# An order of issue that counts table loads, the first Silu behind the last norm, and one operand split on two engines

## The chip, the cores and the metric

The kernel runs on one core of a Trainium2 chip. A core has five engines with queues of their own: TensorE (PE, with its weight loads as PEld), VectorE (DVE), ScalarE (ACT), GpSimd (POOL) and SyncE (SP), which here issues all the DMAs. The metric is the device time of one execution in microseconds (us). The time before is the median of three runs, 3001.66 us (2999.66 to 3004.17). Each trace is one further execution, taken by the hardware profiler.

## The reference

One layer of a streaming encoder, for 2048 prompt tokens and 32 sample tokens of width 1024, in float32. Both groups share the weights, so the kernel treats them as 2080 columns of one transposed matrix.

```python
x = x + rmsnorm(concat(band_attention, gla) @ w_o)       # 8 heads x 64 | 4 heads x 128, gated
x = x + rmsnorm(softmax(rmsnorm(x) @ w_mq @ k.T) @ v @ w_mo)   # 256 memory tokens, 4 heads
x = x + rmsnorm((silu(h @ w_gate) * (h @ w_up)) @ w_down)      # h = rmsnorm(x), hidden 2816
```

`band_attention` is softmax attention of each 64-token chunk over itself and the eight chunks before; `gla` is a gated linear recurrence. Every `rmsnorm(x)` is `x * rsqrt(mean(x * x) + eps) * gain`. The kernel computes the reciprocal root as Exp(-0.5 * Ln(mean + eps)), so a norm needs ScalarE's Ln and Exp; the feed-forward part needs its Silu.

## The kernel before

**Stages.** The input projection (to about 550 us in the trace) works on three blocks of columns. Then attention and the linear recurrence run beside the output projections of earlier blocks. For the output projection the columns are cut into four blocks `BLK` of 512, 512, 512 and 544. Blocks 0 to 2 are projected while later blocks are still in attention; block 3 comes after all attention (about 1150 to 1235 us). Cross-attention follows: scores from 1235 us, and the outputs of eight tiles of 256 columns from about 1410 us. The feed-forward stage starts at about 1625 us and runs over three pairs of column blocks and eleven groups `g` of 256 hidden units, with seven-product forms of the matrix products in gate, up and down.

**Split operands.** The float32 products on PE are made of three fp32r matmuls (`mm3`): each operand is split into a high part, ACT's cast, and a low part, the difference, which DVE or POOL makes. `split` (lines 459 and 460) does this for weights. `split_own` (464 and 465) does it in place, and its second argument picks POOL or DVE for the low part. `load_mov` (line 1098) loads the eight pieces of an output-projection operand (`om`, 128 rows each) from the DRAM buffer `od` and splits them with `split_own(..., True)`, all on POOL.

**The output projection.** `out_proj(b)` (1431) returns three lists of steps: `first` loads and splits the operand, `tile_m` makes one of eight output tiles from `wops` matmuls (1426), and the last list does the norm and the residual. The pieces are taken in the order 4 to 7, 0 to 3: rows 4 to 7 of `od` come from the recurrence (`od<-g_sg`), rows 0 to 3 from attention (`od<-o`, `od<-so`). `score_weights` (1667) prepares the weights for cross-attention's scores: it loads `gs` from `gd` and combines and splits them on ACT, DVE and POOL. It is called ahead of block 3's `first`.

**Cross-attention's norms.** `output(i, pT)` (1839) makes a tile's output with matmuls `mo`, squares and sums it (`n_q`, `n_s`), and calls `rstd` twice, for the norm after cross-attention and for the one before the feed-forward part. `rstd` (1854) is a matmul of ones, an Ln (1858) and an Exp (1859). The scaled rows (`my`, 1868) are stored to `x2d` and `h2d`.

**The feed-forward units.** `gate_up(g)` (2134) makes the gate product with `unit` (PSUM tiles `pg_X`, `pg_Y`, `pg_Z`), applies four Silus (2140), one of them straight from `pg_X`, makes the up product (`pu_X` and so on, to three buffers `up`) and multiplies (2143). At the last column block a preload brings ScalarE's set for Ln and Exp back ahead of the final norm.

**What sets the order.** The order of instructions in each queue is written out by a planner, the class `Order`. `_read` (191) reads the traced instructions, gives each a cost by `_cost`, and collects what it depends on. `_pass` (287) runs a list schedule over the five engines with the tiles' buffers as limits, which it counts by tag. `queue` (403) makes eleven such passes forwards and ten backwards, each taking its priorities from the one before, keeps the shortest and ties the instructions of each engine into that order. ScalarE's functions live in sets, and a table load stands ahead of an activation whose set isn't in place; the planner before doesn't know of these loads.

Of the kernel before, what the change touches and what calls it, by code (L numbers as in the profile page):

```python
# [18 lines left out]
P = 128  # L19
# [28 lines left out]
class Order:  # L48
# [9 lines left out]
    SLOW = 1.0  # L58
    PASSES = 10
    TURN = 280.0  # L60
    ROOM = (208 * 1024, 16 * 1024)

    def __init__(self, tc):
        self.tc = tc
        self.block = tc.nc.cur_bb
        self.edge = mybir.DependencyInfo(mybir.DependencyClass.NoSync, mybir.DependencyReason.DATA)

    @staticmethod
# [122 lines left out]
    def _read(self, traced):  # L191

        self.ops, self.eng, self.dur, self.lat, self.lane, self.prio = [], [], [], [], [], []
        self.pred, self.uses, tile_of = [], [], {}
        self.tiles = []
        log = []
        opened, closed, owner = {}, {}, {}
# [9 lines left out]
        for ins in traced:  # L207
            kind = type(ins).__name__
            eng = str(ins.engine).split(".")[-1]
            if ins.name in opened:  # L210
                p, space, size, right = opened[ins.name]
                lo = max([q[2] for q in stack.values() if q[0] == space and not q[3]], default=0)
                if right:
                    lo = min([q[1] for q in stack.values() if q[0] == space and q[3]], default=self.ROOM[space == PSUM]) - size
                stack[p] = (space, lo, lo + size, right)
                before = [q for q, (s, a, b) in gone.items() if s == space and a < lo + size and lo < b]
                if before:
                    gate[p] = len(self.ops)
                    form = None
                    self._add(None, self.GATE, (0.0, 0.0), 0, 0, sorted({i for q in before for i in inside.get(q, ())}), [])  # L220
            elif ins.name in closed:
                space, lo, hi, _ = stack.pop(closed[ins.name])
                gone = {q: v for q, v in gone.items() if not (v[0] == space and lo <= v[1] and v[2] <= hi)}
                gone[closed[ins.name]] = (space, lo, hi)
            if kind in ("BassTilePoolBoundary", "InstLoadActFuncSet") or eng not in self.ENGINES:
                continue
            outs = [a.bass_ap for a in ins.outs if hasattr(a, "bass_ap")]
            inps = [a.bass_ap for a in ins.ins if hasattr(a, "bass_ap")]
            was, form = form, self._form(eng, outs, inps)
            joined = form is not None and form == was  # L230
            i = len(self.ops) - joined
            pred, use = set(), []
            for aps, wr in ((inps, False), (outs, True)):
                for ap in aps:
                    t = ap.tensor
                    if type(t).__name__ != "Tile":
                        continue
                    k = tile_of.get(t.name)
                    if k is None:
                        k = tile_of[t.name] = len(self.tiles)  # L240
                        self.tiles.append(t)
                        log.append([])
                    if t.space == PSUM:
                        p0, p1, bits, wr_ = 0, P, 1, True
                    else:
                        p0, p1, bits = self._cells(ap)
                        wr_ = wr
                    keep = []
                    for e in log[k]:
                        j, w, q0, q1, b = e  # L250
                        if j != i and (wr_ or w) and q0 < p1 and p0 < q1 and b & bits:
                            pred.add(j)
                        if not (wr_ and j != i and p0 <= q0 and q1 <= p1 and not b & ~bits):
                            keep.append(e)
                    keep.append((i, wr_, p0, p1, bits))
                    log[k] = keep
                    if t.space != DRAM and k not in use:
                        use.append(k)
                        p = owner.get(t.name)
                        inside.setdefault(p, []).append(i)  # L260
                        if p in gate:
                            pred.add(gate[p])
            cost = self._cost(ins, kind, eng, outs, inps)
            if joined:
                self._join(ins, cost, ins.bass_priority, pred, use)
                continue
            if form is not None:
                cost = cost[0] + self.TURN, cost[1]
            self._add(ins, self.ENGINES.index(eng), cost, self._lane(kind, eng, outs + inps), ins.bass_priority, sorted(pred), use)
        n = len(self.ops)  # L270
        self.succ = [[] for _ in range(n)]
# [15 lines left out]
    def _pass(self, prio, back=None):  # L287

        n = len(self.ops)
        eng, dur, lat, lane = self.eng, self.dur, self.lat, self.lane  # L290
        taken = [0.0] * 3
        nxt, prv = (self.succ, self.pred) if back is None else (self.pred, self.succ)
        left = [len(x) for x in prv]
        live = [k for k in range(len(self.tiles)) if self.first[k] is not None]
# [28 lines left out]
        while True:  # L323
            again = True
            while again:
                again = False
                for e, heap in enumerate(ready):
                    while idle[e] and heap:
# [22 lines left out]
                        idle[e] = False  # L351
                        start[i] = now
                        fin = now + dur[i]
                        if lane[i]:
                            fin = max(fin, taken[3 - lane[i]] + dur[i] - 140.0)
                            taken[lane[i]] = fin
# [42 lines left out]
                            parked[g] = []  # L399
        assert done == n, "the order does not work out"  # L400
        return start, end

    def queue(self):
        self._read(self.block.bb.instructions)
# [25 lines left out]
def encoder_step(ctx, tc, ins, outs):  # L430
# [641 lines left out]
    with ExitStack() as ph, ExitStack() as dn:  # L1072
# [22 lines left out]
            return xps[-1].tile([P, 1088], F32, tag="xw", name=name)  # L1095


        def load_mov(src, n, name, order=range(KT)):
            mv = {}
            for k in order:  # L1100
                mv[k] = mp.tile([P, 2, 544], F32R, tag="mov", name=f"{name}_{k}")
                SP.dma_start(mv[k][:, 1, :n].bitcast(F32), src[k * P : (k + 1) * P])
                split_own(mv[k][:, :, :n], True)
            return mv

        def split_k(ks, kraw):
# [321 lines left out]
                    yield  # L1428


        def out_proj(b):
            s, n = BLK[b]
            chunks = even_split(n, 512)
            mv, y, ys, accs = {}, [], [], []
            order = (4, 5, 6, 7, 0, 1, 2, 3)

            def first():
                mv.update(load_mov(od[b], n, f"om{b}", order))
                y.extend(xtile(f"y1_{b}_{j}")[:, : 2 * n].rearrange("p (k n) -> p k n", k=2) for j in range(4))
                ys.extend(y[k // 2][:, k % 2] for k in range(KT))  # L1440
                accs.append(xtile(f"acc1_{b}")[:, : 2 * n].rearrange("p (k n) -> p k n", k=2))
# [225 lines left out]
        def score_weights():  # L1667
# [3 lines left out]
            for k in range(HK):  # L1671
                b11, b12, b22, b21 = (gst.tile([P, 512], F32, tag="gst", name=f"gs{kh}{hf}_{k}") for kh, hf in ((0, 0), (0, 1), (1, 1), (1, 0)))
                for t, (kh, hf) in zip((b11, b12, b22, b21), ((0, 0), (0, 1), (1, 1), (1, 0))):
                    SP.dma_start(t, gd[kh][hf][:, k * 512 : k * 512 + 512])

                def put(i, src, eng=None):
                    split(gT[i][:, 0, k], gT[i][:, 1, k], src, eng)
# [9 lines left out]
                sub(DVE, b21, b21, b11)  # L1687
                SP.dma_start(s6d[:, k * 512 : k * 512 + 512], b21)

        score_weights()  # L1690
        for _ in steps(outp[3][0] + weave(outp[3][1], [partial(values_fold, 2)] + [partial(values_fold, 3)], lead=1.0)):
            pass
        psx.close()
        amm.close()
# [134 lines left out]
        def softmax(pr, ps, n, st, heads):  # L1829
# [5 lines left out]
            for h in range(heads):  # L1835
                c = slice(h * NMEM, h * NMEM + NMEM)
                DVE.tensor_scalar(out=pr[:n, c], in0=pr[:n, c], scalar1=st[:n, 4 + h : 5 + h], scalar2=None, op0=ALU.mult)

        def output(i, pT):
            t0 = i * 256  # L1840
            y = [yp.tile([P, HK, 256], F32, tag="y", name=f"my{i}_{j}") for j in range(2)]
# [10 lines left out]
                    add(DVE, ssq[nm], ssq[nm], sq)  # L1852

            def rstd(nm):
                r = (pd.tile([P, 512], F32, tag="dense", name=f"{nm}{i}") if nm == "n3_" else ptr.tile([P, 512], F32, tag="tr", name=f"{nm}{i}"))[:, :256]
                add(DVE, ssq[nm][:, 0], ssq[nm][:, 0], ssq[nm][:, 1])
                PE.matmul(r, lhsT=ones, rhs=ssq[nm][:, 0], start=True, stop=True)
                ACT.activation(r, r, AF.Ln, bias=eps_t, scale=1.0 / D)
                ACT.activation(r, r, AF.Exp, scale=-0.5)
                return r  # L1860

            def store(dst, m2):
# [151 lines left out]
    with ExitStack() as ph:  # L2014
# [116 lines left out]
        for b, (s, n) in enumerate(CF):  # L2131
            ssqs, silu = {}, []

            def gate_up(g):
                u = gt.tile([P, 2, 2, 348], F32, tag="g", name=f"g{b}_{g}")[:, :, :, :n]
                sg = {q: u[:, q[0], q[1]] for q in QS}
                up = {q: small(up_, "up", f"up{b}_{g}_{q[0]}{q[1]}", 3)[:, :n] for q in QS[:3]}
                X = unit(unit_w(ins["w_ffn_gate"][0], g, f"wg{b}_{g}"), ops, n, f"pg{b}_{g}", sg)
                for q in QS:
                    silu.append(ACT.activation(sg[q], sg[q] if q != (1, 0) else X, AF.Silu))  # L2140
                up[1, 0] = unit(unit_w(ins["w_ffn_up"][0], g, f"wu{b}_{g}"), ops, n, f"pu{b}_{g}", up)
                for q in QS:
                    DVE.tensor_tensor(out=sg[q], in0=sg[q], in1=up[q], op=ALU.mult)  # L2143
                return u
# [297 lines left out]
```

## Time and profile before

| | before |
|---|---|
| median of three runs | 3001.66 us |
| the profiled execution's own time | 3003.11 us |
| its span, first to last instruction | 3001.3 us |
| PE busy | 2932.2 us (98%) |
| DVE busy | 2259.3 us (75%) |
| ACT busy | 1591.5 us (53%) |
| POOL busy | 836.1 us (28%) |
| mean granted TensorE clock | 0.991 |

A row of the timeline has the start and the duration in us, engine, line, operation, output and inputs, the count, and in brackets the idle time before it with what ended it. A row of a group has its count, the busy time, the mean ns of one, and the idle time ahead of it. A row of stretches has the length and the busy time of PE, PEld, DVE, ACT and POOL, the granted clock, and the share and rate of the DMA engines.

### The profile page before, as it was taken

What the parts mean: (1) busy time and instruction counts of PE and PEld (TensorE: products, weight loads), DVE (VectorE), ACT (ScalarE), POOL (GpSimd) and SP (SyncE); (2) the same over time, 40 slices, a digit from 0 to 9 for tenths busy, and PEclk for the clock granted to TensorE, in tenths of its full rate; (3) what the DMA queues carried; (4) which work ended last, traced back from release to release, by engine and by line L of the source; (5) the groups of instructions that cost most, each with busy time, mean ns of one, the idle gap of its engine ahead of it and who ended that gap; (6) DMA issues with size and microseconds to landing.
All of it is one profiled execution on the core that took longest, in us unless ns stands there. A gap on an engine that the chain in (4) does not pass through costs nothing.

```text
span 3001.3 us, 56406 instructions
## 1 busy us (share of the span) xinstructions
PE 2932.2 (98%) x20995; PEld 2755.9 (92%) x20995; DVE 2259.3 (75%) x4173; ACT 1591.5 (53%) x3388; POOL 836.1 (28%) x987
## 2 busy tenths in 40 slices
PE   9999999999999998999999899999999999999997
PEld 7899999888889786878999899999999999999997
DVE  6587877576767777885679877889877778977775
ACT  5555555576767675665445544445433335433343
POOL 0201000456765564212132121114211113311113
PEclk9999999999999998999999999999999999999999
DMA  9567374985877768545994544454554445544434
GB/s 317 201 200 238 118 228 150 303 280 185 269 224 241 241 192 290 172 171 188 339 302 141 161 168 132 167 177 158 182 185 133 131 147 177 179 161 139 134 128 168
DMA packets 431652, 586.24 MB, mean 195 GB/s; under 512 B 48944, under 2 KB 321305, under 8 KB 431345
## 3 DMA queue, kind: packets, MB, share of 16 engines
q1 hardware_dynamic: 431377, 582.64, 59.4%
q8 instruction: 165, 2.70, 0.4%
q14 instruction: 110, 0.90, 0.1%
HBM read 426.46 MB, written 160.33 MB: 196 GB/s over the span
## 4 chain that ended last, share of the span: by engine, by line
PE 91%; DMA 3%; DVE 3%; ACT 1%; POOL 1%; issue 1%; SPq 0%; DVEq 0%; ACTq 0%; POOLq 0%
PE pu_X L500 8%; PE pg_X L500 8%; PE pdX L500 8%; PE mo L500 6%; PE wops L1426 6%; PE pu_Y L500 4%; PE pg_Y L500 4%; PE pdY L500 4%; PE msX L500 3%; PE s L1154 2%; PE pu_Z L500 2%; PE po L1162 2%; PE pg_Z L500 2%; PE pdZ L500 2%; PE pt L1182 2%; PE pdn L500 2%
## 5 line engine op out<-in xcount | busy, mean ns | idle before, releaser
L460 POOL TENSOR_TENSOR u<-g,u 128x692 fp32r<-128x692 f32 (+1 forms) x111 | 198.4, 1793 | 890.9 <-ACT u L459 889.0
L500 PE MATMUL pu_X<-mf,wu_s 128*128 128x346 f32 (+1 forms) x1584 | 275.8, 322 | 7.7 <-DVE up L555 7.7
L500 PE MATMUL pg_X<-mf,wg_s 128*128 128x346 f32 (+1 forms) x1584 | 277.4, 322 | 2.6 <-DVE g L555 1.7
L500 PEld LDWEIGHTS pu_X<-mf,wu_s 128*128 128x128 f32 x1584 | 256.3, 189 | 8.0 <-DVE up L555 8.0
L500 PEld LDWEIGHTS pg_X<-mf,wg_s 128*128 128x128 f32 x1584 | 255.6, 189 | 5.0 <-DVE g L555 2.2
L500 PE MATMUL pdX<-u,wd 128*128 128x346 f32 (+1 forms) x1440 | 233.1, 322 | 0.9 <-POOL u L460 0.9
L500 PEld LDWEIGHTS pdX<-u,wd 128*128 128x128 f32 x1440 | 230.2, 189 | 1.5 <-POOL u L460 1.2
L459 ACT CAST wg_s<-wg_r 128x512 fp32r<-128x512 f32 x231 | 136.5, 620 | 168.4 <-DVE wg_r L552 78.0
L1426 PE MATMUL wops<-om,wo_s 128*128 128x512 f32 (+1 forms) x960 | 217.7, 366 | 7.4 <-POOL om L465 3.9
L459 ACT CAST u<-g 128x692 fp32r<-128x692 f32 (+1 forms) x111 | 84.5, 774 | 237.8 <-PE pdX L500 172.5
L500 PE MATMUL mo<-pT,hT 128*128 128x256 f32 x1536 | 192.3, 285 | 0.7 <-POOL pT L465 0.7
L500 PEld LDWEIGHTS mo<-pT,hT 128*128 128x128 f32 x1536 | 186.7, 192 | 6.5 <-issue 3.3
L460 DVE TENSOR_TENSOR wu_s<-wu_r,wu_s 128x512 fp32r<-128x512 f32 x231 | 168.8, 757 | 22.7 <-ACT wu_s L459 22.1
L460 DVE TENSOR_TENSOR wg_s<-wg_r,wg_s 128x512 fp32r<-128x512 f32 x231 | 158.1, 707 | 36.5 <-ACT wg_s L459 36.4
L459 ACT CAST wu_s<-wu_r 128x512 fp32r<-128x512 f32 x231 | 136.3, 620 | 92.6 <-DVE wu_r L552 39.5
L1426 PEld LDWEIGHTS wops<-om,wo_s 128*128 128x128 f32 x960 | 155.0, 193 | 32.5 <-POOL om L465 6.8
L555 DVE TENSOR_TENSOR acc<-acc,pdX 128x346 f32<-128x346 f32 (+1 forms) x192 | 97.4, 514 | 61.9 <-PE pdX L500 61.7
L500 PE MATMUL pg_Y<-mf,wg_s 128*128 128x346 f32 (+1 forms) x792 | 138.1, 322 | 0.9 <-ACT pg_c L638 0.9
L500 PE MATMUL pu_Y<-mf,wu_s 128*128 128x346 f32 (+1 forms) x792 | 138.2, 322 | 0.7 <-DVE g L2143 0.7
L500 PEld LDWEIGHTS pu_Y<-mf,wu_s 128*128 128x128 f32 x792 | 128.6, 189 | 1.2 <-DVE g L2143 1.0
L500 PEld LDWEIGHTS pg_Y<-mf,wg_s 128*128 128x128 f32 x792 | 128.6, 189 | 1.2 <-ACT pg_c L638 1.2
L1341 POOL TENSOR_TENSOR g_W<-g_W,g_kq 128x128 f32<-128x128 f32 x224 | 107.8, 515 | 67.3 <-ACT g_W L1333 60.0
(561 smaller groups left out, 7188.9 us busy)
## 6 DMA issues: line engine op xcount, KB each, us to landing
wd<-wdd SPq DMA_DIRECT2D x182, 512.0 KB, 5.3
wg_r<-in_w_ffn_gate_dram SPq DMA_DIRECT2D x66, 512.0 KB, 3.9
wu_r<-in_w_ffn_up_dram SPq DMA_DIRECT2D x66, 512.0 KB, 3.9
q<-qd SPq DMA_DIRECT2D x32, 512.0 KB, 5.7
wo_r<-in_w_o_dram SPq DMA_DIRECT2D x64, 256.0 KB, 4.7
wdd<-wds SPq DMA_DIRECT2D x28, 512.0 KB, 7.6
wdd<-wd SPq DMA_DIRECT2D x28, 512.0 KB, 3.8
nb<-nbd SPq DMA_DIRECT2D x16, 640.0 KB, 7.6
```

Of the source, the lines that this page charges most:

```text
L459: ACT.copy(hi, src)
L460: (lo_eng or DVE).tensor_tensor(out=lo, in0=src, in1=hi.bitcast(F32), op=ALU.subtract)
L500: PE.matmul(ps, lhsT=a, rhs=b, start=first and i == 0, stop=last and i == len(seq) - 1, skip_group_check=skip)
L555: eng.tensor_tensor(out=out, in0=a, in1=b, op=ALU.add)
L1154: PE.matmul(ps_out, lhsT=q[:, 2 * i + e, q0 : q0 + nq], rhs=ks[:, e, k0 : k0 + ncol], start=i == 0, stop=i == 1)
L1162: PE.matmul(po[e * 64 : e * 64 + 64, :n], lhsT=v[:kk, j, e * 64 : e * 64 + 64], rhs=prts[e][:kk, j, :n], start=j == 0, stop=j == len(rows) ...
L1182: PE.transpose(ptp[:kk, j, :n], pr[:n, c0 : c0 + kk], ident[:n, :n])
L1341: POOL.tensor_tensor(out=wl, in0=wl, in1=both, op=ALU.mult)
L1426: PE.matmul(ps, lhsT=a, rhs=b, start=i == 0, stop=i == len(seq) - 1)
```

## The change

Four things are changed. The planner gets a constant `LOAD` of 1280 ns: `_read` notes for each activation which set it needs (Ln and Exp one, Silu the other, any other function none), and `_pass` adds `LOAD` when the set changes. The planner gets a method `behind`, which makes it treat an instruction as dependent on earlier ones. With it the four Silus of the first unit (block 0, `g` 0) are put behind the last Exp of cross-attention's norms, and the loads `gs<-gd` behind the last load of the output projection's operand. For block 3, the pieces are taken in the order 0 to 7, `first` is called ahead of `score_weights`, and the low parts are made by DVE and POOL in turn, starting with DVE.

```diff
+    LOAD = 1280.0
...
+            at[ins.name] = i
+            pred.update(at[x] for x in self.hints.get(ins.name, ()))
...
+            self.table[len(self.ops)] = {AF.Ln: 1, AF.Exp: 1, AF.Silu: 2}.get(ins.func, 0) if kind == "InstActivation" else 0
...
+        taken, table = [0.0] * 3, 1 if back is None else 2
...
+                        if self.table.get(i, 0) not in (0, table):
+                            table = self.table[i]
+                            fin += self.LOAD
...
+    def behind(self, late, early):
+        for x in late:
+            self.hints.setdefault(x.ins.name, []).extend(y.ins.name for y in early)
...
-        def load_mov(src, n, name, order=range(KT)):
+        def load_mov(src, n, name, order=range(KT), both=False, ld=None):
...
-                split_own(mv[k][:, :, :n], True)
+                ld.append(SP.dma_start(mv[k][:, 1, :n].bitcast(F32), src[k * P : (k + 1) * P]))
+                split_own(mv[k][:, :, :n], not both or len(mv) % 2 == 0)
...
-            order = (4, 5, 6, 7, 0, 1, 2, 3)
+            order = range(KT) if b == NB - 1 else (4, 5, 6, 7, 0, 1, 2, 3)
...
-                    SP.dma_start(t, gd[kh][hf][:, k * 512 : k * 512 + 512])
+                    issue_order.behind([SP.dma_start(t, gd[kh][hf][:, k * 512 : k * 512 + 512])], om_loads[-1:])
...
+        for it in outp[3][0]:
+            it()
         score_weights()
-        for _ in steps(outp[3][0] + weave(outp[3][1], ...)):
+        for _ in steps(weave(outp[3][1], ...)):
...
+                normed = ACT.activation(r, r, AF.Exp, scale=-0.5)
...
+                if b == 0 and g == 0:
+                    issue_order.behind(silu, [normed])
```

More of the change, by code (lines that the diff above doesn't have):

```diff
@@ L65, in __init__ @@
         self.block = tc.nc.cur_bb
+        self.hints = {}
         self.edge = mybir.DependencyInfo(mybir.DependencyClass.NoSync, mybir.DependencyReason.DATA)
@@ L194, in _read @@
         self.pred, self.uses, tile_of = [], [], {}
+        self.table = {}
+        at = {}
         self.tiles = []
@@ L290, in _pass @@
         eng, dur, lat, lane = self.eng, self.dur, self.lat, self.lane
-        taken = [0.0] * 3
+        taken, table = [0.0] * 3, 1 if back is None else 2
         nxt, prv = (self.succ, self.pred) if back is None else (self.pred, self.succ)
@@ L1095, in xtile @@
             return xps[-1].tile([P, 1088], F32, tag="xw", name=name)
-        def load_mov(src, n, name, order=range(KT)):
-            mv = {}
+        def load_mov(src, n, name, order=range(KT), both=False, ld=None):
+            mv, ld = {}, [] if ld is None else ld
             for k in order:
                 mv[k] = mp.tile([P, 2, 544], F32R, tag="mov", name=f"{name}_{k}")
-                SP.dma_start(mv[k][:, 1, :n].bitcast(F32), src[k * P : (k + 1) * P])
-                split_own(mv[k][:, :, :n], True)
+                ld.append(SP.dma_start(mv[k][:, 1, :n].bitcast(F32), src[k * P : (k + 1) * P]))
+                split_own(mv[k][:, :, :n], not both or len(mv) % 2 == 0)
             return mv
@@ L1428, in mm3_steps @@
                     yield
+        om_loads = []
         def out_proj(b):
@@ L1434, in out_proj @@
             mv, y, ys, accs = {}, [], [], []
-            order = (4, 5, 6, 7, 0, 1, 2, 3)
+            order = range(KT) if b == NB - 1 else (4, 5, 6, 7, 0, 1, 2, 3)
             def first():
-                mv.update(load_mov(od[b], n, f"om{b}", order))
+                mv.update(load_mov(od[b], n, f"om{b}", order, b == NB - 1, om_loads))
                 y.extend(xtile(f"y1_{b}_{j}")[:, : 2 * n].rearrange("p (k n) -> p k n", k=2) for j in range(4))
@@ L1688, in score_weights @@
                 SP.dma_start(s6d[:, k * 512 : k * 512 + 512], b21)
+        for it in outp[3][0]:
+            it()
         score_weights()
-        for _ in steps(outp[3][0] + weave(outp[3][1], [partial(values_fold, 2)] + [partial(values_fold, 3)], lead=1.0)):
+        for _ in steps(weave(outp[3][1], [partial(values_fold, 2)] + [partial(values_fold, 3)], lead=1.0)):
             pass
@@ L1837, in softmax @@
                 DVE.tensor_scalar(out=pr[:n, c], in0=pr[:n, c], scalar1=st[:n, 4 + h : 5 + h], scalar2=None, op0=ALU.mult)
+        normed = None
         def output(i, pT):
@@ L1854, in rstd @@
             def rstd(nm):
+                nonlocal normed
                 r = (pd.tile([P, 512], F32, tag="dense", name=f"{nm}{i}") if nm == "n3_" else ptr.tile([P, 512], F32, tag="tr", name=f"{nm}{i}"))[:, :256]
@@ L1858, in rstd @@
                 ACT.activation(r, r, AF.Ln, bias=eps_t, scale=1.0 / D)
-                ACT.activation(r, r, AF.Exp, scale=-0.5)
+                normed = ACT.activation(r, r, AF.Exp, scale=-0.5)
                 return r
```

## The prediction

> **What bounds the kernel now.** First the page: the busy times with their shares of the span, and the chain that ended last.
>
> ```profile
> PE 2932.2 (98%) x20995; PEld 2755.9 (92%) x20995; DVE 2259.3 (75%) x4173; ACT 1591.5 (53%) x3388; POOL 836.1 (28%) x987
> PE 91%; DMA 3%; DVE 3%; ACT 1%; POOL 1%; issue 1%; SPq 0%; DVEq 0%; ACTq 0%; POOLq 0%
> ```
>
> TensorE is busy for 2932.2 of 3001.3 us (the end of the last stage below) and is 91% of the chain, so an edit that adds or removes no matmul can win only from the 69.1 us in which PE stands still, and from stretches in which it runs slowly. The second view says where these are: the busy time of PE, PEld, DVE, ACT and POOL in six stages, then the granted clock.
>
> ```profile
> 0.00:1136.00 1136.00, 1112.82 (x9542) 1001.15 (x9544) 809.54 (x1744) 725.82 (x1747) 407.55 (x710) 1.00 0.71 226
> 1136.00:1195.00 59.00, 45.04 (x218) 34.60 (x214) 40.35 (x58) 30.80 (x68) 26.72 (x19) 0.83 0.91 302
> 1195.00:1625.00 430.00, 426.96 (x2814) 379.70 (x2813) 312.78 (x592) 236.00 (x487) 106.70 (x62) 1.00 0.67 226
> 1625.00:1730.00 105.00, 93.97 (x559) 90.83 (x559) 90.39 (x152) 59.59 (x105) 16.16 (x11) 0.95 0.51 160
> 1730.00:2960.00 1230.00, 1227.21 (x7698) 1224.59 (x7697) 982.57 (x1591) 521.73 (x947) 260.55 (x167) 1.00 0.48 159
> 2960.00:3001.30 41.30, 26.18 (x177) 25.00 (x175) 23.65 (x41) 17.57 (x39) 18.41 (x19) 0.88 0.22 69
> ```
>
> Length less PE gives the idle time: 23.2, 14.0, 3.0, 11.0, 2.8 and 15.1 us. Two short stages hold 25.0 of it at a lowered clock (0.83 and 0.95): the start of the last block's output projection (1136 to 1195) and the change from cross-attention to the feed-forward stage (1625 to 1730). The change works at these two. The third view is who PE waits for there, with total, count and longest.
>
> ```profile
> PE wops L1426 <- POOL om L465: 3.9, 7, 0.8
> PE pu_X L500 <- DVE up L555: 7.7, 1, 7.7
> ```
>
> In the first place seven waits on POOL's operand split; in the second one of 7.7 us on DVE.
>
> **Part 1: the last block's operand on two engines.** In order of time: start, duration, engine, line, count. These rows are of the stretch around the operand `om`.
>
> ```profile
> 1147.45 0.37 SPq L1415 DMA_DIRECT2D od<-g_sg  x1
> 1151.11 4.99 SPq L1102 DMA_DIRECT2D om<-od  x8
> 1157.24 12.23 POOL L465 TENSOR_TENSOR om<-om 128x544 fp32r<-128x544 f32 x8 [12.32 <-DMA om<-od]
> 1163.44 3.54 DVE L460 TENSOR_TENSOR wo_s<-wo_r,wo_s 128x512 fp32r<-128x512 f32 x2 [3.86 <-ACT wo_s L459]
> 1169.13 4.70 SPq L1674 DMA_DIRECT2D gs<-gd  x6
> 1170.88 11.16 PE L1426 MATMUL wops<-om,wo_s 128*128 128x272 f32 x72 [0.53 <-DVE y L1467]
> ```
>
> ACT's halves are done early; POOL makes the low halves of eight pieces in 12.23 us, 1.53 each, PE takes three matmuls per piece as they come, and only at 1170.88 does it run freely. The next rows price the pieces: POOL's, a DVE operation of the same 128x544 form with two SBUF inputs, and DVE's weight splits in this stretch.
>
> ```profile
> L465 POOL TENSOR_TENSOR om<-om 128x544 fp32r<-128x544 f32 x8 | 12.2, 1558 | 12.3 <-DMA om<-od 12.3
> L555 DVE TENSOR_TENSOR acc<-acc,sqa 128x544 f32<-128x544 f32 x1 | 0.7, 714 | 0.0
> L460 DVE TENSOR_TENSOR wo_s<-wo_r,wo_s 128x512 fp32r<-128x512 f32 x9 | 10.4, 1179 | 3.9 <-ACT wo_s L459 3.9
> ```
>
> Four pieces move to DVE at 0.71 instead of 1.56. If the two engines worked at once, POOL's four would set the end, 4 x 1.56 = 6.2, and 6.0 us would go. But the two wo_s splits at 1163.44 took 3.54, 1.77 each, while POOL worked. DVE and POOL hold each other up, so I add them: 4 x (1.56 + 0.71) = 9.1, and 3.1 us go. [...]
>
> The block order changes too: pieces 0 to 3, the attention rows, come first. Before, all eight loads go out at 1151.11, behind od<-g_sg (1147.45), the store of the rows 4 to 7. The last store of attention rows went out 3.1 us ahead of that:
>
> ```profile
> 1144.32 0.33 SPq L1281 DMA_DIRECT2D od<-so  x1
> ```
>
> Four loads could go right behind the g_sg store, at 1147.8, 3.3 us earlier, if the planner puts them there; the other four need the g_sg store and gain less. They are the same eight DMAs, now traced ahead of the 16 loads gs<-gd, the four stores s6d and the kernel's other score-weight work. The added wait of gs<-gd on the last om load costs nothing: in the queue they already stand 13 us behind it (1169.13 against 1156.10). I take half, 1.7, between 0 and 3.3.
>
> The clock: 72 matmuls at 1170.88 took 11.16; the first row below gives 34.7 / 268 = 0.129 each later, so 9.3, and 1.9 are lost to half clock after the thin stretch. I take half, 0.9, between 0 and 1.9.
>
> What is late next: the next rows are the later wops matmuls and two stretches in order.
>
> ```profile
> L1426 PE MATMUL wops<-om,wo_s 128*128 128x272 f32 x268 | 34.7, 288 | 0.7 <-ACT wo_s L459 0.7
> 1160.00:1182.00 22.00, 17.53 (x97) 15.38 (x98) 8.56 (x11) 8.81 (x16) 12.04 (x9) 0.77 1.01 341
> 1182.00:1195.00 13.00, 8.56 (x45) 6.78 (x44) 12.93 (x18) 8.71 (x17) 3.15 (x2) 1.00 0.97 307
> ```
>
> From 1182 DVE is full (12.93 of 13.0) with splits of wo, wov and the score weights, and PE idles 4.4 us. A PE that comes earlier meets this wall earlier; but DVE has 13.4 us free in the stretch ahead (22.0 less 8.6), and the moved pieces take 2.9. If the planner moves that work forward the gain stays, otherwise nearly all is given back. I keep four fifths: 0.8 x (3.1 + 1.7 + 0.9) = **4.5 us**, from -1 (2.9 us more on a full DVE, less the 1.9 of clock) to 11.2 (6.0 + 3.3 + 1.9).
>
> **Part 2: the table loads and the first Silu.** Cross-attention's last norms (Ln and Exp, lines 1858 and 1859) now run among the first units' Silus (line 2140). The rows below are the table loads by line, and one pair of them in time.
>
> ```profile
> L1858 ACT ACT_TABLE_LOAD  x3: 1283/1283/1283, 1675.9 to 1699.8; - x3
> L1859 ACT ACT_TABLE_LOAD  x3: 1283/1283/1283, 1678.3 to 1705.4; - x3
> L2140 ACT ACT_TABLE_LOAD  x5: 1283/1283/1283, 1637.9 to 2573.3; - x5
> 1678.28 1.28 ACT L1859 ACT_TABLE_LOAD   x1
> 1679.57 0.37 ACT L1859 ACTIVATE n<-n 128x256 f32<-128x256 f32 x1
> ```
>
> Three Ln and three Exp each reload, and so does the Silu after them (one of the five of line 2140); of these only the Silu load of 1637.9 remains, later, when every Silu stands behind the last Exp. Seven loads go, 7 x 1.283 = 9.0 us of ACT. ACT itself has room; what matters is who waits.
>
> ```profile
> 1677.00:1686.00 9.00, 8.43 (x50) 7.67 (x49) 3.98 (x8) 7.20 (x12) 0.00 (x0) 1.00 0.11 37
> 1699.20:1713.00 13.80, 13.05 (x65) 12.71 (x66) 9.32 (x19) 9.60 (x17) 0.00 (x0) 0.82 0.20 60
> ```
>
> DVE stands still for 5.0 us in the first stretch and 4.5 in the second, in which ACT loads tables. In between the norm work comes late on POOL and DVE and PE does nothing: the 7.7 us. The end of that wait, in time:
>
> ```profile
> 1694.17 4.00 POOL L555 TENSOR_TENSOR my<-my,x1r 128x512 f32<-128x512 f32 x3 [2.14 <-DVE my L1868]
> 1699.20 3.85 PE L500 MATMUL pu_X<-mf,wu_s 128*128 128x348 f32 x12 [7.67 <-DVE up L555]
> ```
>
> So DVE, 1625 to 1677 at 49.84 of 52.0 (below), is the tight engine, and its 9.5 idle us are what can be won. PE has 11.0 idle us here, and its pu_X group at 1699.20 took 3.85 where the next row gives 12 x 66.7 / 384 = 2.1, so 1.8 of half clock. At most 12.8 us can go.
>
> ```profile
> L500 PE MATMUL pg_X<-mf,wg_s 128*128 128x348 f32 x384 | 66.7, 322 | 0.8 <-DVE g L555 0.8
> 1621.64 4.06 PE L500 MATMUL mo<-pT,hT 128*128 128x256 f32 x31
> 1625.00:1677.00 52.00, 51.77 (x322) 50.88 (x322) 49.84 (x79) 34.06 (x64) 5.63 (x4) 1.00 0.47 140
> ```
>
> What the hint adds: every Silu of unit 0 waits for the last Exp. On ACT the queue behind them holds weight casts that the planner may put ahead. PE waits for the PSUM bank that gate product X keeps for its Silu, and for up's X and the three `up` buffers, which wait for the multiply behind it. The order counts banks by tag, three for these: from the last mo matmul at 1625.7, PE has the gate unit and the up unit of g = 0 (7 x 12 x 0.174 = 14.6 each) and the four X products of the next gate (8.4), 37.6 us, until 1663. The norms' work in 1625 to 1713:
>
> ```profile
> L1868 DVE SCALAR_TENSOR_TENSOR my<-my,g_post_mem,n 128x256 f32<-128x256 f32 x16 | 6.8, 472 | 0.0
> L555 DVE TENSOR_TENSOR n_s<-n_s,n_q 128x512 f32<-128x512 f32 x9 | 7.2, 802 | 0.2
> L555 POOL TENSOR_TENSOR my<-my,x1r 128x512 f32<-128x512 f32 x8 | 11.2, 1406 | 70.1 <-DMA wu_r<-in_w_ffn_up_dram 34.1 <-DVE my L1868 33.6 <-ACT wu_s L459 2.4
> L460 DVE TENSOR_TENSOR wg_s<-wg_r,wg_s 128x512 fp32r<-128x512 f32 x19 | 13.4, 731 | 2.6 <-ACT wg_s L459 2.6
> L460 DVE TENSOR_TENSOR wu_s<-wu_r,wu_s 128x512 fp32r<-128x512 f32 x18 | 13.5, 776 | 2.8 <-ACT wu_s L459 2.7
> ```
>
> If the norms go first, 6.8 + 7.2 + 11.2 (POOL in the way of DVE) = 25.2 us, done by 1651: no stall. If all 37 weight splits (26.9) go first too, 1678: a stall of 15. The planner sees both and needs only part of the splits by then; I take 4.8, nearer the first, and 12.8 - 4.8 = **8 us**, from -2.2 (12.8 - 15) to 12.8.
>
> [...]
>
> **Part 3: LOAD in the order.** 1.28 us agrees with the rows, once per change of set, though an Ln and Exp pair costs two. The Ln, Exp and Silu in the feed-forward blocks also reload, but there PE idles 2.8 us in 1230, so nothing is to be won. The priorities of all instructions are worked out anew, so other stages may shift: 0, with +-4 from the 23 us idle before 1136.
>
> **Sum.** The profiled execution took 3003.11 us (1.8 outside its span). 3003.1 - 4.5 - 8 = 2990.6. It lies 1.4 above the median 3001.66; against the runs, **2989 us**. Own range 2981 to 2996.
>
> **Rivals.**
> *One part only.* DVE, already 95% and 99% full in both places, gives one gain back: PE waits for wo_s and g instead of om, or for the Silu at 1663 instead of for up at 1691. For: the full DVE rows. Against: its idle time (13.4, 9.5) just ahead. Time: 3001.7 - 4.5 to - 8, mostly 2994 to 2998.
> *Nothing to see.* The order puts the om loads where they were, the stall is only renamed, and the rest shifts: 2998 to 3003. For: gs<-gd already stood behind om, and PE is 98% busy. Against: seven loads vanish whatever the order.
> *Slower.* The Silu becomes the gate. It decides as soon as the last norm's Exp ends more than 37.6 + 12.8 = 50.4 us after the last mo matmul, so after 1676, against 1707.0 now and 1651 to 1678 by the sums above. At 1690, the weight casts and 20 us of residual work ahead of it, PE would idle 27 us (from 1663) in place of 12.8 lost: 3001.7 + 14.2 - 4.5 = 3011. For: DVE at 49.84 of 52.0 leaves the norm no free room. Against: the planner knows the wait and ranks the norm by it.
>
> **Chances.** Forecast 0.50, one part only 0.27, nothing 0.13, slower 0.10. Under 0.2% (6 us) a measurement of this kernel can't tell a change from none, so faster means below 2995.7: all but a little of the first and half of the second, 0.67; the rest of these and the third, 0.23; slower 0.10. The range runs from 2979 (both parts at their upper bounds would give 3001.7 - 11.2 - 12.8 = 2977.7) to 3003 (the second rival's end, with the slower case left out).
>
> **What would show it.** Right: no table load on 1858 and 1859, one of line 2140 before 2000 us; DVE without the 5.0 and 4.5 us gaps; PE's longest wait in the second place under 5 us; four of the om splits on DVE and the span from the first to the last under 10 us. Wrong: PE waiting longest for ACT's g or sg at about 1663; wops waiting for wo_s for longer than now; or the idle time before 1136 changed by more than either part.

## The result, and the profile after

The changed kernel takes 3006.27 us (median of 22 runs, 3000.86 to 3010.04), the kernel before 3000.98 (22 runs, 2996.74 to 3008.27): a ratio of 1.0014, 95% interval 1.0008 to 1.0020. It is 0.14% slower where 2989 was forecast. That is less than the 0.2% under which the prediction held that a change can't be told from none. But the interval leaves out 1, so a small loss is there, and 3006.27 lies above the whole stated range (2979 to 3003). The profiled execution took 3008.49.

The page of the changed kernel, busy times and chain, looks like that of before:

```profile
PE 2935.7 (98%) x20995; PEld 2761.6 (92%) x20995; DVE 2271.4 (76%) x4177; ACT 1595.4 (53%) x3390; POOL 831.5 (28%) x983
PE 90%; DVE 3%; DMA 3%; ACT 2%; issue 1%; SPq 0%; POOL 0%; DVEq 0%; ACTq 0%; POOLq 0%
```

The same stages as before the change (length; PE, PEld, DVE, ACT, POOL busy; clock; DMA):

```profile
0.00:1136.00 1136.00, 1112.52 (x9511) 1000.67 (x9513) 806.48 (x1739) 728.13 (x1749) 407.34 (x706) 1.00 0.71 226
1136.00:1195.00 59.00, 50.32 (x289) 42.34 (x286) 43.36 (x66) 27.82 (x61) 21.21 (x18) 0.84 0.86 281
1195.00:1625.00 430.00, 421.57 (x2747) 373.31 (x2747) 317.88 (x587) 234.46 (x483) 110.13 (x63) 0.99 0.68 228
1625.00:1730.00 105.00, 96.55 (x580) 95.08 (x579) 91.03 (x159) 64.63 (x112) 16.41 (x12) 0.95 0.52 166
1730.00:2960.00 1230.00, 1223.31 (x7670) 1219.91 (x7669) 983.99 (x1583) 521.04 (x944) 255.94 (x166) 1.00 0.47 159
```

In both places of the change PE idles less (8.7 us in place of 14.0, and 8.5 in place of 11.0), but in the two long stages it idles more (8.4 for 3.0, and 6.7 for 2.8). These windows are fixed in time, and the changed kernel's work lies up to 3.2 us later in them; the table of stretches below follows the work itself. ACT is busier in 1625 to 1730: 64.63 in place of 59.59. Of these 5.0 us, 1.3 are one more table load; the rest is other work that fell into the window. The table loads of the whole kernel by line (2162 is the Silu, 1880 and 1881 the norm's Ln and Exp, 2318 and 2319 those at the end of a feed-forward block):

```profile
L2162 ACT ACT_TABLE_LOAD x7 | 9.0, 1283 | 0.1
L2318 ACT ACT_TABLE_LOAD x4 | 5.1, 1283 | 0.1
L2319 ACT ACT_TABLE_LOAD x4 | 5.1, 1283 | 0.1
L1880 ACT ACT_TABLE_LOAD x3 | 3.8, 1283 | 0.1
L1881 ACT ACT_TABLE_LOAD x3 | 3.8, 1283 | 0.1
```

No load went, and the Silu's five became seven. One of the two more is in this place, which has nine loads where it had eight; the other is at the finish of block 1 (2551 us), where LOAD alone has one more too. ACT's rows in time show the order, and PE's waits what it did:

```profile
1670.39 1.28 ACT L2162 ACT_TABLE_LOAD   x1
1671.69 0.49 ACT L2162 ACTIVATE g<-g 128x348 f32<-128x348 f32 x1
...
1674.29 1.28 ACT L1880 ACT_TABLE_LOAD   x1
...
1676.05 1.28 ACT L1881 ACT_TABLE_LOAD   x1
...
1678.09 1.28 ACT L1880 ACT_TABLE_LOAD   x1
...
1679.86 1.28 ACT L1881 ACT_TABLE_LOAD   x1
...
1681.54 1.28 ACT L2162 ACT_TABLE_LOAD   x1
...
1684.75 0.60 ACT L474 CAST wg_s<-wg_r 128x512 fp32r<-128x512 f32 x1
```

```profile
PE pg_X L515 <- ACT wg_s L474: 5.1, 1, 5.1
PE pu_Z L515 <- DVE g L2167: 3.1, 1, 3.1
```

The Silu of 1671.69 belongs to unit 1 (`g` = 1): the order written out for ACT has one Silu of unit 1, two norms, three more Silus of unit 1, the last norm, and only then unit 0. The hint binds unit 0 alone, and the planner let unit 1 overtake it. Six loads, 7.7 us, now stand in 12.4 us ahead of a weight cast; PE waits 5.1 us for that cast (its `pg_X` starts at 1685.41) where it waited 7.7 for `up` before.

### The profile page after: what moved, and what is told of

Its sections match the earlier page's. It is cut to its first block, busy times and chain, and to the rows that moved or that the text cites. A ratio compares the mean times of both kernels' runs of the same rounds, so it can differ in the third digit from the quotient of the medians.

```text
span 3006.7 us, 56443 instructions
## 1 busy us (share of the span) xinstructions
PE 2935.7 (98%) x20995; PEld 2761.6 (92%) x20995; DVE 2271.4 (76%) x4177; ACT 1595.4 (53%) x3390; POOL 831.5 (28%) x983
## 4 chain that ended last, share of the span: by engine, by line
PE 90%; DVE 3%; DMA 3%; ACT 2%; issue 1%; SPq 0%; POOL 0%; DVEq 0%; ACTq 0%; POOLq 0%
PE pu_X L515 8%; PE pg_X L515 8%; PE pdX L515 8%; PE mo L515 6%; PE wops L1441 6%; PE pu_Y L515 4%; PE pg_Y L515 4%; PE pdY L515 4%; PE msX L515 3%; PE s L1169 2%; PE pu_Z L515 2%; PE po L1177 2%; PE pdZ L515 2%; PE pg_Z L515 2%; PE pt L1197 2%; PE pdn L515 2%
```

## Experiments

Each was timed beside the kernel before on the same chip (5 to 11 runs of each, 24 to 33 of the kernel before). The kernel before had a median of 3000.04 beside LOAD alone, the operand alone and the two hints, 3002.91 beside the split, the order and the last two rows, and 3001.64 beside the others. So compare the ratios, not the medians.

| kernel | median us | ratio to before, 95% interval |
|---|---|---|
| LOAD alone | 3004.17 | 1.0014 (1.0005 to 1.0023) |
| operand alone | 3000.85 | 1.0007 (0.9998 to 1.0016) |
| of it, split alone | 3002.64 | 0.9999 (0.9989 to 1.0008) |
| of it, order alone | 3003.23 | 1.0004 (0.9995 to 1.0013) |
| hint on unit 0 alone | 3003.48 | 1.0011 (1.0003 to 1.0020) |
| hint on units 0 and 1 | 2996.51 | 0.9989 (0.9980 to 0.9998) |
| all parts, two units | 3000.07 | 1.0001 (0.9992 to 1.0010) |
| LOAD alone, set kept | 3000.62 | 1.0000 (0.9991 to 1.0008) |
| LOAD per function | 2992.28 | 0.9971 (0.9960 to 0.9983) |
| two units, set kept | 2992.56 | 0.9970 (0.9960 to 0.9981) |
| LOAD per function, operand | 2997.24 | 0.9980 (0.9970 to 0.9989) |
| LOAD per function, two units | 2991.36 | 0.9968 (0.9956 to 0.9981) |

The next table is worked out from the traces: the length in us of eight stretches of PE's work, cut at the last matmul of the sample's recurrence (`gs_tt`), the first `msX`, `mo` and `pg_X`, the first `pdn` of blocks 0, 1 and 2, and the end. Behind the bar stands how many us of each of the first seven ran at half clock (a granted clock of 0.5).

```
                          start  o-proj scores  outs  block0 block1 block2  end  | half clock
before                    1030.7  204.6  175.3  214.9  447.8  446.7  444.5  36.8 |  6.8 20.5 3.4 0.0 10.2 0.0 0.0
after                     1031.1  202.1  176.6  218.9  445.6  449.6  446.0  36.9 | 10.2 20.5 0.0 6.8 10.2 0.0 0.0
LOAD alone                1027.7  204.2  175.3  214.9  444.7  451.2  445.9  36.9 |  3.4 20.5 3.4 0.0 13.7 3.4 0.0
operand alone             1025.1  202.3  176.7  214.9  446.6  446.7  444.5  36.9 |  3.4 17.1 3.4 0.0 10.2 0.0 0.0
split alone               1029.0  202.8  176.7  216.5  447.5  446.7  444.5  36.9 | 10.2 17.1 3.4 3.4  6.8 0.0 0.0
order alone               1028.3  202.1  176.2  216.4  447.7  446.6  444.5  36.8 | 13.7 17.1 0.0 3.4 10.2 0.0 0.0
hint on unit 0            1024.4  204.7  175.3  214.9  450.2  446.7  444.5  36.9 |  0.0 20.5 3.4 0.0 20.5 0.0 0.0
hint on two units         1026.9  204.4  175.3  214.9  440.3  446.7  444.5  36.8 |  3.4 20.5 3.4 0.0  6.8 0.0 0.0
all parts, two units      1027.0  202.8  176.7  214.9  439.9  451.0  446.0  36.9 |  6.8 20.5 3.4 0.0  6.8 3.4 0.0
LOAD alone, set kept      1027.4  203.2  174.8  218.8  445.1  446.9  446.0  36.9 |  3.4 23.9 0.0 3.4 10.2 0.0 0.0
LOAD per function         1026.1  204.4  175.3  214.9  440.6  445.6  446.0  35.8 |  3.4 17.1 3.4 0.0  0.0 0.0 0.0
two units, set kept       1027.2  203.8  174.8  216.4  440.1  445.7  444.5  36.9 |  6.8 23.9 0.0 3.4  6.8 0.0 0.0
per function, operand     1028.0  204.0  177.5  216.5  442.2  445.7  446.0  35.8 |  3.4 23.9 6.8 3.4  3.4 0.0 0.0
per function, two units   1026.2  203.5  174.8  216.5  440.8  445.7  446.0  35.8 |  3.4 23.9 0.0 3.4  6.8 0.0 0.0
```

Two columns show how it is to be read. Block 2 has 444.5 in seven kernels and 446.0 in the other seven to 0.1 us, so a difference there is one of the order. "outs" has 214.9 in the seven traces where no half clock fell into it and 216.4 or 216.5 in five of the others, with one window of it; I take that difference for chance. The other two are longer by waits as well: LOAD alone with the set kept (218.8) has 2.2 us more of idle time there, the changed kernel (218.9, two windows) 0.7.

By the same cuts, PE's idle time before and after the change is 14.8 and 13.4 us in the output projection, 1.6 and 4.2 in scores, 0.7 and 1.5 in outs, 11.9 and 9.3 in block 0, 2.0 and 4.7 in block 1, 0.0 and 1.1 in block 2. The two places of the change won 4.0 us of idle time, and the four other stretches lost 7.2.

### The hint

```diff
 # hint on unit 0 alone: no LOAD, operand as before
+                if b == 0 and g == 0:
+                    issue_order.behind(silu, [normed])
 # hint on units 0 and 1
+                if b == 0 and g < 2:
+                    issue_order.behind(silu[-4:], [normed])
```

> Only the hint is added: unit 0's four Silus behind the last norm's Exp. Theory N: unit 1's Silus stand among the norms, at least as many table loads as before between 1625 and 1730, and PE waits there for gate work of ACT or DVE in place of the 7.7 us wait; gain of at most 1 us or loss up to 3: 3000 to 3004. Rival R: no difference beside that of the reshuffled order, a loss of 4 to 6 with its place outside 1625 to 1730. Rival P (the prediction's part 2 as it was worked out): 2993.

> As the hint alone, but the Silus of units 0 and 1 both stand behind the last norm's Exp, so that no Silu comes between two norms. Theory N: seven table loads go (no load on the lines of Ln and Exp of the norm, one Silu load before 2000 us), DVE's gaps of 5.0 and 4.5 us close, and the time is that of part 2 of the prediction, 2993, give or take 3. Rival S (a Silu that waits for the norm is the gate): PE waits over 10 us for unit 0's gate products, 3001 to 3011. Rival R: 3001 to 3006 whatever the loads do, since PE's 11.0 idle us in 1625 to 1730 are renamed, not removed.

On unit 0 alone the hint makes block 0's stretch 2.4 us longer (450.2 for 447.8). All but 0.3 of this is busy time: 20.5 us of half clock fell into it in place of 10.2. It need not be chance of this one trace, since the mean granted clock of its 11 runs is 0.9892 where the kernel before has 0.9912. It has nine loads in this place, as theory N had it; PE waits longest there for the sums of the last norm (6.3 us), not for gate work as theory N said.

On two units the stretch is 7.5 us shorter: 5.5 of idle time (6.4 for 11.9) and 2.0 of busy time, with one half-clock window fewer. The table loads between 1600 and 1760 us are here one in place of eight:

```profile
L2160 ACT ACT_TABLE_LOAD x1 | 1.3, 1283 | 0.0
```

All in all the kernel has 14 loads where before has 21: seven went, as the prediction had it. What stays is PE's wait, the longest in this place now, for the sums of the last norm:

```profile
PE n L1877 <- DVE n_s L570: 5.7, 1, 5.7
```

So theory N holds for the loads. Rival S falls: PE waits for no Silu. Rival R falls too, since idle time went. The median gained 3.3 us (0.0011 of 3000; 0.6 to 6.0), under the 7 expected and under the 7.5 of its trace; with the set kept, below, it is 9.0. The hint also puts the norms ahead of the Silus, so how much of the gain is the loads' and how much the new order's was not separated.

### All parts with the wider hint

> The changed kernel with one difference: the Silus of units 0 and 1, not of unit 0 alone, stand behind the last norm's Exp. Theory N with sums (LOAD +4.1, operand about 0, hint on unit 0 +3.4, hint on two units -3.5, each against a before of 3000.0): 3000.6, so 5 to 7 below the changed kernel. Rival M (the changed kernel's parts disturb each other, and what one gains another takes): no better than the changed kernel, 3005 to 3007.

This is the changed kernel with `g < 2` in place of `g == 0`. Block 0's stretch is 439.9 in place of 445.6, and the median 3000.07: the wider hint takes back the loss against the kernel before (a ratio of 1.0001 for 1.0014, 3.9 us), but that is less than a quarter of the 17.3 us to the forecast, and the kernel gains nothing over before. Its block 1 has 451.0 for 446.7 and block 2 has 446.0 for 444.5, as in the next kernel.

### LOAD

```diff
 # LOAD alone: no hint, operand as before
+    LOAD = 1280.0
...
```

> Only the table load of 1280 ns is added to the order's costs; the operand of the last block and the gate functions stay as before. Theory N (the hint is too narrow: it binds unit 0's Silus, unit 1's go ahead of them among the norms, so no load goes and a Silu stall is added): LOAD alone does little, within 3 us of before (3001). Rival R (the reshuffled order as such costs the time, by the finish of block 0, where in the changed kernel two Ln/Exp pairs stand back to back at 2096 to 2105 and first n_ps is 5.0 us later): LOAD alone already costs 4 to 6 us, 3005 to 3007, and the finish of block 0 shows the same block of table loads.

It loses 4.2 us of median (1.5 to 6.9): more than theory N's 3, and the size and the place that rival R named. In the trace block 0's stretch gains 3.1, block 1 loses 4.5 (2.7 of idle time and 1.7 of busy time, with a half-clock window) and block 2 1.4, together 2.8. The loss of block 1 is at the finish of block 0, which runs inside block 1's first units. First ACT before the change, then with LOAD alone:

```profile
2091.86 1.28 ACT L2294 ACT_TABLE_LOAD   x1
...
2093.69 1.28 ACT L2295 ACT_TABLE_LOAD   x1
...
2097.30 0.45 ACT L638 COPY pg_c<-pg_Y 128x346 f32<-128x346 f32 x1 [0.23 <-PE pg_Y L500]
2097.77 1.28 ACT L2294 ACT_TABLE_LOAD   x1
...
2099.60 1.28 ACT L2295 ACT_TABLE_LOAD   x1
...
2101.91 0.45 ACT L638 COPY pg_c<-pg_X 128x346 f32<-128x346 f32 x1
```

```profile
2088.77 1.28 ACT L2314 ACT_TABLE_LOAD   x1
...
2091.18 0.45 ACT L653 COPY pg_c<-pg_Y 128x346 f32<-128x346 f32 x1
...
2092.49 1.28 ACT L2315 ACT_TABLE_LOAD   x1
...
2094.25 1.28 ACT L2314 ACT_TABLE_LOAD   x1
...
2096.09 1.28 ACT L2315 ACT_TABLE_LOAD   x1
...
2098.25 0.45 ACT L653 COPY pg_c<-pg_X 128x346 f32<-128x346 f32 x1
```

The planner charges once for a change between "Ln or Exp" and "Silu", so a second pair right behind the first seems free. In both traces a load of 1.28 us stands ahead of each of the four, in either order. Packed, three loads stand between the copy of `pg_Y` and that of `pg_X`, 7.1 us apart where they were 4.6, and PE waits 2.6 us for the latter where it waited 0.6 (the same wait stands in the changed kernel's trace; the rows are before, then LOAD alone):

```profile
PE pg_X L500 <- ACT pg_c L638: 0.6, 1, 0.6
```

```profile
PE pg_X L515 <- ACT pg_c L653: 2.6, 1, 2.6
PE pdY L515 <- ACT u L474: 1.3, 1, 1.3
```

Two kernels test this. One leaves the order at this place and takes loads away: behind a block's last Silu the set that has both functions is loaded once. The other leaves the loads and gives the planner the count that the rows show, a load for each: 1 for Ln, 2 for Exp, 4 for Silu, with 3 for the set at the start.

```diff
 # LOAD alone, set kept
             if not last:
+                with tc.issue_after(silu[-1].ins):
+                    ACT.preload_act_table_set("natural_log_exp_and_others")
                 down(NG - 1, held[-1], (1, 0))
 # LOAD per function
...
-            self.table[len(self.ops)] = {AF.Ln: 1, AF.Exp: 1, AF.Silu: 2}.get(ins.func, 0) if kind == "InstActivation" else 0
+            self.table[len(self.ops)] = {AF.Ln: 1, AF.Exp: 2, AF.Silu: 4}.get(ins.func, 0) if kind == "InstActivation" else 0
...
-        taken, table = [0.0] * 3, 1 if back is None else 2
+        taken, table = [0.0] * 3, 3 if back is None else 4
+        silu = min((i for i, t in self.table.items() if t == 4), default=n)
...
-                        if self.table.get(i, 0) not in (0, table):
-                            table = self.table[i]
+                        need = self.table.get(i, 0)
+                        if need and not need & table:
+                            table = 3 if back is not None and i < silu and need < 4 else need
                             fin += self.LOAD
```

> LOAD alone, as in the first experiment, with the same order of ScalarE's instructions at the finish of block 0, but the table set that holds Ln and Exp is loaded once behind the block's last Silu, so that three of the four loads in the pack of two Ln/Exp pairs go (22 loads become 19). Theory F (LOAD alone loses its 4 us because its order packs both pairs ahead of the copy pg_c, and each of the pack's loads keeps that copy and PE waiting): pg_X waits for pg_c at most 0.6 us, no half clock behind it, 2999 to 3001. Rival R (the loss is the reshuffled order's as such): 3003 to 3005 as with LOAD alone.

> LOAD alone again, but the order counts as the trace shows it: once a Silu has run, an Ln and an Exp each cost a load (before, one load for a change between the pair and Silu). The order then no longer puts the two pairs of block 0's finish back to back; a copy pg_c and casts stand between them. Theory F: 2999 to 3001.5, the wait for pg_c at 0.6 to 1.5. Rival R: 3003 to 3005.

With the set kept, block 1's stretch falls from 451.2 to 446.9, the wait for `pg_c` is gone (only the 1.3 of `pdY` stands there), and the median is that of before (1.0000 for 1.0014). Theory F holds: the loads in the pack cost it. The 1.4 us of block 2 stay: all seven kernels that count loads have 445.9 or 446.0 there, all seven that don't have 444.5. Where LOAD is charged per change of set, 1.1 of it is one pause of PE ahead of a `pdZ` matmul, for which the profile shows no wait; why the order has it stays open.

LOAD per function did far better than expected: 2992.28, 8.7 us (5.1 to 12.0) under before. It has as many loads as before (21), in nearly the same sequence of Silus and norms, but block 0's stretch is 440.6 (4.6 us less of idle time, and no half clock in place of 10.2). PE's longest waits there (the second view) are a fraction of the 7.7 us; the first view has the loads:

```profile
L2162 ACT ACT_TABLE_LOAD x2 | 2.6, 1283 | 0.0
L1880 ACT ACT_TABLE_LOAD x3 | 3.8, 1283 | 0.1
L1881 ACT ACT_TABLE_LOAD x3 | 3.8, 1283 | 0.1
```

```profile
PE pdX L517 <- ACT u L476: 2.3, 1, 2.3
PE pg_X L517 <- DVE g L572: 1.3, 1, 1.3
```

Which step of the new order removes the stall was not traced. It is one order of issue, so a lucky one isn't ruled out; with the operand added, below, the stall stays away too (idle 7.4 us in block 0).

### Both remedies

> The hint on two units alone (no LOAD, the operand as before), and the set of Ln and Exp loaded once behind the last Silu of each block but the last: 14 loads become 10. Theory F: at the finish of block 0 the wait for pg_c is only 0.6 us before, so this adds at most 1 us to the 3.5 that the hint on two units gained: 2995.5 to 2997. Rival (ScalarE's loads delay PE's copies in the whole stretch, not in the pack alone): 2 to 4 us more, 2992 to 2994.5.

> LOAD counted per function, and units 0 and 1 behind the last norm's Exp; operand as before. Both won in the same 11.0 idle us and 1.8 of half clock between 1625 and 1730, so they don't add up: 2991 to 2994. If their gains were of different places they would add up to 12 us: 2988.

Two units with the set kept take 2992.56, LOAD per function with two units 2991.36, and their block 0 has 440.1 and 440.8: like each remedy alone, so they win the same microseconds and do not add up. That keeping the set added 5.7 us to the median of two units alone, where at most 1 was expected, is not borne out by the traces (440.1 and 445.7 against 440.3 and 446.7). The median lies where the rival had it (2992 to 2994.5), but these two stretches show 1.2 us of it; I take the rest for the spread between runs, which was not shown. LOAD per function and these two kernels beat the one before by 0.3%.

### The operand

The diffs leave out LOAD and the hint; "split alone" keeps `both=True` for block 3; "order alone" keeps all low halves on POOL and has the loads `gs<-gd` behind the last `om` load.

```diff
 # split alone
-                mv.update(load_mov(od[b], n, f"om{b}", order))
+                mv.update(load_mov(od[b], n, f"om{b}", order, b == NB - 1, om_loads))
 # order alone
+            order = range(KT) if b == NB - 1 else (4, 5, 6, 7, 0, 1, 2, 3)
+        for it in outp[3][0]:
+            it()
         score_weights()
```

> Only the last block's operand is changed (half of the low halves on DVE, blocks in order 0 to 7, loads traced ahead of the score weights, their reads put behind). Theory N: the 2.2 us that the changed kernel gained from 1136 to 1235 stay, and nothing is lost elsewhere: 2998 to 3000. Rival R: any change of order costs later what it gains here: 3001 to 3006.

> Of the operand's change only the split: half of the low halves on DVE; block order, place of the loads and reads of the score weights as before. Theory P (the prediction's term): the waits of wops for POOL's om fall from 3.9 us to about 1 and 2 to 3 us are gained up to the end of the output projection, 2997.5 to 2999. Theory D (DVE, which is full from 1182 on, gives it back in the scoring stage; the operand's whole change gained 2.3 there and kept 0.9): 2999 to 3001.

> Of the operand's change only the order: blocks 0 to 7 instead of 4 to 7 first, loads traced ahead of the score weights, their reads behind the last of the loads; all low halves stay on POOL. Theory P (the prediction's term of 1.7 for earlier loads): 2998 to 2999.5. Theory D (the GLA chain behind the rows 4 to 7 is put off instead: g_o waits 2.5 for DVE's at and the store od<-g_sg goes out about 4 us later, as in the changed kernel, so that nothing is won): 3000 to 3003.

> LOAD counted for each Ln, Exp and Silu that needs its own load, and the operand's change; no hint. Sum of the two measured alone (-8.7 and about +0.4 against before): 2992 to 2994. If the loss of LOAD as it was written came from the reshuffled order by chance, and the gain of LOAD per function too, a further shuffle by the operand undoes it: 2998 to 3004.

None of the first three operand kernels differs measurably from before. With the whole operand part the output projection is 2.3 us shorter (202.3 for 204.6): 1.0 of idle time and 1.3 of busy time, with one half-clock window fewer. Scores are 1.4 longer, 1.2 of it idle time. PE's waits from 1125 to 1240 with the operand alone:

```profile
PE g_o L1405 <- DVE at L570: 2.5, 1, 2.5
PE ss L1169 <- DVE sks L1126: 2.2, 1, 2.2
PE wops L1441 <- ACT om L479: 2.2, 2, 1.7
PE wops L1441 <- DVE y L1484: 1.4, 2, 0.8
PE wops L1441 <- POOL om L480: 1.0, 1, 1.0
```

The 3.9 us for POOL's `om` fell to 1.0, while the wait for DVE's `at` grew from 1.2 to 2.5, and waits for DVE's `sks` and ACT's `om` came in. Why ACT's: in the changed kernel, where ACT's `om` costs 1.8, the planner did the attention rows first, and the store of the recurrence's rows went out at 1151.86, 4.4 us later than before, so the last four loads left at 1156.40, 5.3 later than all eight did:

```profile
1151.86 0.37 SPq L1430 DMA_DIRECT2D od<-g_sg  x1
...
1156.40 3.22 SPq L1117 DMA_DIRECT2D om<-od  x4
...
1163.21 0.72 DVE L480 TENSOR_TENSOR om<-om 128x544 fp32r<-128x544 f32 x1
...
1163.95 3.63 POOL L480 TENSOR_TENSOR om<-om 128x544 fp32r<-128x544 f32 x2 [6.84 <-ACT om L479]
...
1164.59 1.78 DVE L480 TENSOR_TENSOR om<-om 128x544 fp32r<-128x544 f32 x1
```

Added to LOAD per function the operand did not help (a ratio of 0.9980 for 0.9971, with intervals that overlap), and scores took 177.5 for 175.3, 1.4 of it busy time with a half-clock window more. The 2997.24 lie between the two times that were expected. By the ratio the kernel is 6.0 us (3.3 to 9.0) faster than before, so the expected sum of 8.3 isn't ruled out, and the run decides nothing.

## Why the prediction was wrong

**Part 2, -8, failed at its first step.** "Seven loads go" rests on "when every Silu stands behind the last Exp"; the hint orders only unit 0's, and unit 1's Silus need no product of unit 0's. In place of seven loads fewer, one more came there (nine for eight), and block 0's stretch gained 2.2 us (445.6 for 447.8). "Seven loads vanish whatever the order", said against the second rival, is the same error: it took the intent of a hint for what it binds. With two units bound the seven loads went and the trace lost 7.5 us there, near the 8, but the median gained only 3.3 (0.6 to 6.0). The stall set against it (4.8, a choice between 0 and 15) came, but as 5.7 us at the norm's matmul, not at the Silu at 1663. Nor did the loads have to go: counted per function, all 21 stayed and the stall of 7.7 us went.

LOAD counts an Ln followed by an Exp as one load. The traces differ: once a Silu had run, each of the seven pairs in the kernel before took two, 1283 ns each; with the set that has both loaded ahead, the finish of block 0 ran its two pairs without a further load. The prediction noted that "an Ln and Exp pair costs two" and drew nothing from it.

**Part 3, 0 with +-4, was mis-sized and misplaced.** LOAD alone costs 4.2 (1.5 to 6.9). The prediction looked for shifts ahead of 1136 and dismissed the feed-forward blocks because PE idles only 2.8 us there, "so nothing is to be won". Little was, but there was something to lose: at the finish of block 0 the packed loads made PE wait 2.6 us for a copy where it had waited 0.6.

**Part 1, -4.5, came to nothing that can be measured.** The operand alone lies between 0.6 us faster and 4.8 slower. The term of 3.1 for the split shows in the wait for POOL's `om` (3.9 to 1.0). That DVE and POOL hold each other up was right: a DVE piece took 1.78 beside POOL and 0.72 without, and POOL's eight pieces before the change took between 1.33 and 1.80. But the sum in the term, 1.56 + 0.71 for a pair, was an estimate that no run shows: side by side the pieces took 1.78 on DVE and 1.82 on POOL (two in 3.63). The term of 1.7 for earlier loads failed: it held the store at 1147.45, which moved. The term of 0.9 for the clock is not shown either way: the output projection has one half-clock window fewer in the three operand kernels, but not in the changed kernel. And "I keep four fifths" failed: scoring took back 1.4 of 2.3.

**The rivals.** "Slower" had the side but not the cause, since no Silu became the gate. "Nothing to see" had its words, "the stall is only renamed", in both places. Of the signs named ahead, those of being right failed at once: loads stood on the norm's lines, and PE's longest wait in the second place was 5.1 us. None of the three signs of being wrong came: PE waited longest for a weight cast, `wops` waited less for DVE's `wo_s` (1.2 us for 2.1), and the idle time before 1136 stayed (23.5 for 23.2). They looked for other failures than the one that happened.

**What stays open.** Of the 5.4 us between the two profiled executions, 3.3 are half clock in "outs", which I take for chance; the medians are 5.3 apart all the same. The mean granted clock of their runs, 0.9905 for the changed kernel and 0.9912 for before (its 33 runs beside the first four experiments), makes about 2 us of that by an estimate (0.0007 of 3000). How the rest divides over LOAD and hint from run to run was not shown.

## What to carry to other kernels

A hint that orders instructions binds those it names: ask which neighbours of the same kind may overtake them, and count the loads in the order that comes out, since that can be read before anything runs. A wrong price in a planner can be worse than none: here a charge per change of set packed three loads between two copies that TensorE needed, and the kernel whose planner counted as the traces show, per function, was 0.29% faster than the one before. An engine that is busy half of the time can still stop TensorE: ScalarE, busy 53% of the span in the changed kernel, made it wait 5.1 us there for a weight cast behind six loads in its queue, and 2.6 us for a copy behind three with LOAD alone.

## What was not expected of the hardware

The half clock seems a matter of chance over much of the run. In every trace its stretches last 3.41 us or a multiple of it (apart from the one in which the trace ends), and 3.41 of them cost 1.6 us of busy PE (216.5 for 214.9 in "outs"). In the changed kernel's trace a stretch follows 32 thin matmuls (128x32) without any idle time of PE; the rows are before, in and behind it, PE busy throughout, the clock third from the end:

```profile
1493.40:1496.70 3.30, 3.30 (x32) 3.30 (x31) 3.12 (x6) 0.00 (x0) 0.00 (x0) 1.00 0.96 344
1496.80:1503.40 6.60, 6.60 (x30) 6.42 (x31) 3.67 (x9) 4.54 (x9) 2.72 (x3) 0.50 1.06 361
1503.60:1510.00 6.40, 6.40 (x55) 6.40 (x55) 6.26 (x4) 3.48 (x6) 5.88 (x3) 1.00 0.80 252
```

Half clock fell into the stretch of these matmuls ("outs" in the table) in 7 of the 14 traces, one of each kernel, 3.4 or 6.8 us of it, and not in the others. The wait of 2.6 us at block 0's finish was followed by 3.4 us of it with LOAD alone and with all parts and two units, but by none in the changed kernel.
